# Strassen's seven products in the MLP down projection of a Griffin-style decoder layer

## Chip, cores and metric

The kernel runs on one core of a Trainium2 chip. The metric is device time in microseconds (us); the time of the kernel before is the median of three runs.

## The reference, cut to what matters

One decoder layer on 512 tokens of width 2048: three token mixers, a gated merge, and a squared-ReLU MLP with 8192 hidden features. All of it is float32. Only the MLP matters here:

```python
D_MODEL = 2048
SEQ = 512
D_FF = 4 * D_MODEL
...
        x = x + merged @ w_out[l]

        h2 = rms_norm(x, mlp_norm_w[l])
        x = x + jnp.square(jax.nn.relu(h2 @ w_mlp_up[l])) @ w_mlp_down[l]
```

## The kernel before

**Precision.** Each float32 factor is split into a high part (rounded to the fp32r type) and a low part (the rest). A product is three matmuls, high x high, high x low and low x high (`mm3`, lines 110 to 113). A weight tile arrives as `raw`, 128 partitions x 2 x 512 float32 (512 KB), by one load from SyncE's queue; ScalarE casts it to `whi` (line 100) and VectorE subtracts to get `wlo` (line 102). The rings hold 4 `raw`, 3 `whi` and 3 `wlo` tiles.

**MLP.** It runs in 8 blocks of 1024 hidden features (lines 923 to 941). The up product of a block is two calls of `feat_major`: 4 accumulators of 128 features x 512 tokens, 8 weight groups of 256 input features, so 24 matmuls of 128x128 by 512 columns for each weight tile. After each half, ScalarE applies relu (`rl`, line 929), VectorE squares (line 930), ScalarE casts to `u_h` (line 933), and VectorE subtracts to `u_l` (line 934). The factor of the second norm is left out of `u` and put into `r2` (one number for each token). The down product is four calls of `tok_major`, one for each 512 output columns: 4 accumulators of 128 tokens x 512 columns, 4 weight groups of 256 hidden features, again 24 matmuls for each weight tile. VectorE then adds each accumulator, times `r2`, to the residual `x1` (line 939). In the last block the results are stored right after that (line 941).

**Space.** Two pools of four PSUM tiles of 128 x 512: `acc` for the accumulators of both products, and `sm` for small things of the attention and for transposes. `T` is a pool of 75 tiles of 128 x 512 float32 in SBUF; in the MLP `x1` takes 16 of them, the normed activations `h2` 32, and `u_h` and `u_l` 16.

**Order.** The program is traced in the order written; the framework adds the semaphores and chooses each engine's order, in which an instruction can go ahead of an earlier one that is not yet ready. Once chosen, the order of each engine is fixed. The matmuls of one block's up and down products follow each other.

## Time and profile before

| what | us |
|---|---|
| median of three runs | 2969.28 (2967.07 to 2970.88) |
| span of the profiled execution | 2966.8 |
| TensorE busy | 2946.1 (99%) |
| VectorE busy | 1145.6 (39%) |
| ScalarE busy | 872.2 (29%) |
| MLP, first to last matmul (1569.6 to 2962.6 in the span) | 1393.0 |

For the profiled execution the profile gives its span only, from the first to the last recorded instruction; it is 2.5 us below the median of the runs. PE is TensorE's matmuls and PEld its weight loads, DVE is VectorE, ACT is ScalarE, POOL is GpSimd, SP is SyncE, whose queue issues the loads. A matmul's own duration (0.39 us) overlaps the next one's, so the spacing of the starts, not the duration, tells what one costs. In a row of a group, the text behind "|" gives busy us, the mean ns of one, and the idle time of the engine before them with what ended it.

### The profile page before, as it was taken

To read this page: it belongs to the slowest core of one execution; us is meant where nothing else is said; L and a number is where in the kernel's file an instruction comes from. 1 tells how busy PE (TensorE), PEld (TensorE's weight loads), DVE (VectorE), ACT (ScalarE), POOL (GpSimd) and SP (SyncE) were. 2 spreads that over 40 slices of the span, in tenths; PEclk is the share of its full clock that TensorE was granted. 3 is DMA by queue.
4 is the path that set the end of the run, shared out by engine and by line. 5 is a ranking of instruction groups with operands and counts; after the bars stand their busy time and mean duration, and the time that the engine had idled before them with its cause. 6 is when DMAs were issued, how large, how long until landed. Compare 5 with 4: busy or idle time off the path is not lost.

```text
span 2966.8 us, 33995 instructions
## 1 busy us (share of the span) xinstructions
PE 2946.1 (99%) x14046; PEld 2405.0 (81%) x14046; DVE 1145.6 (39%) x1697; ACT 872.2 (29%) x1352; POOL 125.1 (4%) x134
## 2 busy tenths in 40 slices
PE   8999999999999999999999999999999999999999
PEld 6988777777888888888888888888888888888887
DVE  6435666645322323343323333333332332433333
ACT  6334443344222222222323213122221312222131
POOL 0001111100000100010000000000000000000000
PEclk9999999999999999999999999999999999999999
DMA  6423222122333333333333333333333333333333
GB/s 228 119 71 87 65 68 66 54 65 65 95 97 100 93 99 100 93 98 111 113 119 93 99 94 99 98 94 100 95 97 100 93 99 100 93 100 96 96 100 106
DMA packets 198837, 285.97 MB, mean 96 GB/s; under 512 B 19575, under 2 KB 76698, under 8 KB 198682
## 3 DMA queue, kind: packets, MB, share of 16 engines
q1 hardware_dynamic: 189312, 281.16, 31.9%
q10 hardware_dynamic: 9370, 2.64, 0.4%
q8 instruction: 110, 1.80, 0.2%
q14 instruction: 45, 0.37, 0.0%
HBM read 279.16 MB, written 4.60 MB: 96 GB/s over the span
## 4 chain that ended last, share of the span: by engine, by line
PE 96%; DVE 1%; DMA 1%; POOL 1%; ACT 1%; issue 0%; ACTq 0%; SPq 0%; POOLq 0%; DVEq 0%
PE fa L111 20%; PE fa L112 20%; PE fa L113 20%; PE ta L113 10%; PE ta L111 10%; PE ta L112 10%; PE ps L802 1%; PE dps L795 1%; PE ps L810 1%; PE ps L789 0%; PE yy L754 0%; PE sp L493 0%; PE lp L561 0%; PE lp L517 0%; DVE wlo L102 0%
## 5 line engine op out<-in xcount | busy, mean ns | idle before, releaser
L102 DVE TENSOR_TENSOR wlo<-raw,whi 128x1024 fp32r<-128x1024 f32 (+2 forms) x520 | 626.7, 1206 | 1518.4 <-ACT whi L100 1514.8
L100 ACT CAST whi<-raw 128x1024 fp32r<-128x1024 f32 (+2 forms) x520 | 536.9, 1033 | 1682.7 <-PE fa L112 977.2
L111 PE MATMUL fa<-h_h,whi 128*128 128x512 f32 x2336 | 927.5, 397 | 0.0
L113 PE MATMUL fa<-h_h,wlo 128*128 128x512 f32 x2336 | 912.4, 391 | 0.0
L112 PE MATMUL fa<-h_l,whi 128*128 128x512 f32 x2336 | 912.4, 391 | 0.0
L111 PEld LDWEIGHTS fa<-h_h,whi 128*128 128x128 f32 x2336 | 438.6, 188 | 98.2 <-issue 11.3
L113 PEld LDWEIGHTS fa<-h_h,wlo 128*128 128x128 f32 x2336 | 438.5, 188 | 92.3 <-issue 1.0
L112 PEld LDWEIGHTS fa<-h_l,whi 128*128 128x128 f32 x2336 | 438.9, 188 | 86.6 <-issue 1.2
L111 PE MATMUL ta<-whi,u_h 128*128 128x512 f32 x1024 | 398.3, 389 | 0.0
L112 PE MATMUL ta<-wlo,u_h 128*128 128x512 f32 x1024 | 398.3, 389 | 0.0
L113 PE MATMUL ta<-whi,u_l 128*128 128x512 f32 x1024 | 398.3, 389 | 0.0
L113 PEld LDWEIGHTS ta<-whi,u_l 128*128 128x128 f32 x1024 | 192.2, 188 | 39.9
L111 PEld LDWEIGHTS ta<-whi,u_h 128*128 128x128 f32 x1024 | 192.2, 188 | 39.9
L112 PEld LDWEIGHTS ta<-wlo,u_h 128*128 128x128 f32 x1024 | 192.2, 188 | 39.9
L939 DVE SCALAR_TENSOR_TENSOR x<-ta,r,x 128x512 f32<-128x512 f32 x128 | 93.0, 747 | 44.2 <-PE ta L113 44.2
L111 PE MATMUL ta<-whi,m_h 128*128 128x512 f32 x256 | 99.9, 390 | 0.0
L113 PE MATMUL ta<-whi,m_l 128*128 128x512 f32 x256 | 99.6, 389 | 0.0
L112 PE MATMUL ta<-wlo,m_h 128*128 128x512 f32 x256 | 99.6, 389 | 0.0
L111 PE MATMUL fa<-ob_h,whi 128*128 128x512 f32 x256 | 99.6, 389 | 0.0
L112 PE MATMUL fa<-ob_l,whi 128*128 128x512 f32 x256 | 99.6, 389 | 0.0
L113 PE MATMUL fa<-ob_h,wlo 128*128 128x512 f32 x256 | 99.6, 389 | 0.0
L882 POOL TENSOR_TENSOR mg<-mg,sg 128x512 f32<-128x512 f32 x32 | 49.6, 1580 | 639.6 <-DVE sg L881 639.6
(279 smaller groups left out, 1912.0 us busy)
## 6 DMA issues: line engine op xcount, KB each, us to landing
raw<-in_w_mlp_up_dram SPq DMA_DIRECT2D x128, 512.0 KB, 3.7
raw<-in_w_mlp_down_dram SPq DMA_DIRECT2D x128, 512.0 KB, 3.8
raw<-in_w_in_dram SPq DMA_DIRECT2D x112, 512.0 KB, 3.6
raw<-in_w_in_dram SPq DMA_DIRECT2D x120, 256.0 KB, 3.0
raw<-in_w_out_dram SPq DMA_DIRECT2D x32, 512.0 KB, 3.8
raw<-in_w_mem_kv_dram SPq DMA_DIRECT2D x16, 512.0 KB, 4.9
raw<-in_p_swa_dram SPq DMA_DIRECT2D x12, 512.0 KB, 3.8
raw<-in_p_dn_dram SPq DMA_DIRECT2D x12, 512.0 KB, 3.8
```

The source lines that it names most:

```text
L100: nc.scalar.copy(out=hi, in_=raw)
L102: nc.vector.tensor_tensor(out=lo, in0=raw, in1=hi.bitcast(F32), op=ALU.subtract)
L111: nc.tensor.matmul(ps, lhsT=l_hi, rhs=r_hi, start=first, stop=False)
L112: nc.tensor.matmul(ps, lhsT=l_hi, rhs=r_lo, start=False, stop=False)
L113: last_mm[0] = nc.tensor.matmul(ps, lhsT=l_lo, rhs=r_hi, start=False, stop=last)
L795: nc.tensor.matmul(dps[rs, :], lhsT=R[rs, t, :], rhs=tmp, start=True, stop=True)
L802: nc.tensor.matmul(ps2, lhsT=kd[rs, t, :], rhs=delta, start=True, stop=True)
L810: nc.tensor.matmul(ps3[rs, :], lhsT=PT[rs, t, :], rhs=delta, start=True, stop=True)
L882: nc.gpsimd.tensor_tensor(out=merged[kt], in0=merged[kt], in1=sg[j], op=ALU.add)
L939: nc.vector.scalar_tensor_tensor(out=x1[t, c], in0=accs[t], scalar=r2[:, t:t + 1], in1=x1[t, c], op0=ALU.mult, op1=ALU.add)
```

## The change

In blocks 0 to 6 the down product (512 tokens x 1024 features by 1024 features x 2048 columns) is cut into halves in all three dimensions, 2x2 blocks of 256 x 512 and of 512 x 1024, and done by Strassen's method: seven block products of sums and differences. `SEVEN` lists for each product which activation blocks are combined, which weight blocks, and to which output blocks it goes with which sign. A weight block that is a sum is loaded as two `raw` tiles for each part and added by VectorE in place, ahead of the split. The activations are now kept unsplit as `u` (tiles of 128 x 2 x 256), with relu and square both on ScalarE; they are combined (`a_s`, VectorE) and split (`a_h` on ScalarE, `a_l` on VectorE) once for each product. A product is done in two units, one for each 512 columns: two accumulators from the `sm` pool, 24 matmuls, then an accumulation on VectorE into one or two output blocks for each of two token tiles, with `r2` or its negative and an add or a subtract for the sign.

Five of the seven products combine two weight blocks, five combine two activation blocks, and five go to two output blocks (twelve targets in all).

`merged_order` traces one up step of the next block (one weight tile, 24 matmuls), then one down unit of this block, and so on: 16 up steps with 14 units. Block 0's up product runs alone ahead, and block 7's down product stays the plain one behind, on four `sm` accumulators. The rest of the diff removes comments and names the ring's size of 4 (`RAWS`).

```diff
+RAWS = 4
+SEVEN = (
+    (((0, 0, 1),), ((0, 1, 1), (1, 1, -1)), ((0, 1, 1), (1, 1, 1))),
+    (((1, 1, 1),), ((1, 0, 1), (0, 0, -1)), ((0, 0, 1), (1, 0, 1))),
+    (((0, 0, 1), (1, 1, 1)), ((0, 0, 1), (1, 1, 1)), ((0, 0, 1), (1, 1, 1))),
+    (((1, 0, 1), (1, 1, 1)), ((0, 0, 1),), ((1, 0, 1), (1, 1, -1))),
+    (((0, 0, 1), (0, 1, 1)), ((1, 1, 1),), ((0, 0, -1), (0, 1, 1))),
+    (((1, 0, 1), (0, 0, -1)), ((0, 0, 1), (0, 1, 1)), ((1, 1, 1),)),
+    (((0, 1, 1), (1, 1, -1)), ((1, 0, 1), (1, 1, 1)), ((0, 0, 1),)),
+)
...
     NE = 8
-    for e_ in range(NE):
-        u = []
+    nr2 = const.tile([P, 4], F32, name="nr2")
+    nc.vector.tensor_scalar(out=nr2, in0=r2, scalar1=-1.0, scalar2=None, op0=ALU.mult)
+    sgn = {1: (ALU.add, r2), -1: (ALU.subtract, nr2)}
+    def up_steps(e_, u):
         for half in range(2):
-            accs = feat_major([rows(w_up, 256 * g, e_ * 1024 + half * 512, 512) for g in range(8)], h2, 4)
+            accs = [acc_tile("fa") for _ in range(4)]
+            for g in range(8):
+                hi, lo = wload(rows(w_up, 256 * g, e_ * 1024 + half * 512, 512), 512)
+                for j in range(4):
+                    for k in range(2):
+                        ah, al = h2[2 * g + k]
+                        c = slice(j * P, (j + 1) * P)
+                        mm3(accs[j], hi[:, k, c], lo[:, k, c], ah, al, g == 0 and k == 0, g == 7 and k == 1)
+                if g < 7:
+                    yield
             for j in range(4):
-                rl = T("rl")
-                nc.scalar.activation(out=rl, in_=accs[j], func=AF.Relu)
-                nc.vector.tensor_tensor(out=rl, in0=rl, in1=rl, op=ALU.mult)
-                hh = T("u_h", F32R)
-                hl = T("u_l", F32R)
-                nc.scalar.copy(out=hh, in_=rl)
-                nc.vector.tensor_tensor(out=hl, in0=rl, in1=hh.bitcast(F32), op=ALU.subtract)
-                u.append((hh, hl))
-        for c in range(4):
-            accs = tok_major([rows(w_dn, e_ * 1024 + 256 * g, c * 512, 512) for g in range(4)], u, 512, 4)
+                p_, k = 2 * half + j // 2, j % 2
+                for h in range(2):
+                    if k == 0:
+                        u[p_, h] = T("u", shape=(P, 2, 256))
+                    nc.scalar.activation(out=u[p_, h][:, k, :], in_=accs[j][:, h * 256:(h + 1) * 256], func=AF.Relu)
+                    if k == 1:
+                        nc.scalar.activation(out=u[p_, h], in_=u[p_, h], func=AF.Square)
+            yield
+    def split(src):
+        hh = T("a_h", F32R, (P, 2, 256))
+        hl = T("a_l", F32R, (P, 2, 256))
+        nc.scalar.copy(out=hh, in_=src)
+        nc.vector.tensor_tensor(out=hl, in0=src, in1=hh.bitcast(F32), op=ALU.subtract)
+        return hh, hl
+    def down_units(e_, u):
+        for at, bt, ct in SEVEN:
+            act = []
+            for i in range(2):
+                t0, k0, _ = at[0]
+                src = u[2 * k0 + i, t0]
+                if len(at) == 2:
+                    t1, k1, s1 = at[1]
+                    both = T("a_s", shape=(P, 2, 256))
+                    nc.vector.tensor_tensor(out=both, in0=src, in1=u[2 * k1 + i, t1], op=sgn[s1][0])
+                    src = both
+                act.append(split(src))
+            for c in range(2):
+                accs = [sm("da") for _ in range(2)]
+                for i in range(2):
+                    raws = []
+                    for k0, m0, _ in bt:
+                        raw = wp.tile([P, 2, 512], F32, tag="raw", bufs=RAWS, name="raw")
+                        nc.sync.dma_start(out=raw, in_=rows(w_dn, e_ * 1024 + k0 * 512 + i * 256, m0 * 1024 + c * 512, 512))
+                        raws.append(raw)
+                    if len(bt) == 2:
+                        nc.vector.tensor_tensor(out=raws[0], in0=raws[0], in1=raws[1], op=sgn[bt[1][2]][0])
+                    hi, lo = wsplit(raws[0], 512)
+                    ah, al = act[i]
+                    for t in range(2):
+                        for k in range(2):
+                            cs = slice(t * P, (t + 1) * P)
+                            mm3(accs[t], ah[:, k, cs], al[:, k, cs], hi[:, k, :], lo[:, k, :], i == 0 and k == 0, i == 1 and k == 1)
+                for t in range(2):
+                    for t0, m0, s0 in ct:
+                        tt, cc_ = 2 * t0 + t, 2 * m0 + c
+                        nc.vector.scalar_tensor_tensor(out=x1[tt, cc_], in0=accs[t], scalar=sgn[s0][1][:, tt:tt + 1], in1=x1[tt, cc_], op0=ALU.mult, op1=ALU.add)
+                yield
+    def merged_order(first_, second):
+        live = [first_, second]
+        while live:
+            for gen in list(live):
+                if next(gen, "end") == "end":
+                    live.remove(gen)
+    u = {}
+    for _ in up_steps(0, u):
+        pass
+    for e_ in range(NE - 1):
+        nu = {}
+        merged_order(up_steps(e_ + 1, nu), down_units(e_, u))
+        u = nu
+    us = {key: split(t_) for key, t_ in u.items()}
+    e_ = NE - 1
+    for c in range(4):
+        accs = [sm("da") for _ in range(4)]
+        for g in range(4):
+            hi, lo = wload(rows(w_dn, e_ * 1024 + 256 * g, c * 512, 512), 512)
             for t in range(4):
-                nc.vector.scalar_tensor_tensor(out=x1[t, c], in0=accs[t], scalar=r2[:, t:t + 1], in1=x1[t, c], op0=ALU.mult, op1=ALU.add)
-                if e_ == NE - 1:
-                    nc.sync.dma_start(out=out[0, t * P:(t + 1) * P, c * 512:(c + 1) * 512], in_=x1[t, c])
+                for k in range(2):
+                    ah, al = us[g, t // 2]
+                    cs = slice((t % 2) * P, (t % 2 + 1) * P)
+                    mm3(accs[t], ah[:, k, cs], al[:, k, cs], hi[:, k, :], lo[:, k, :], g == 0 and k == 0, g == 3 and k == 1)
+        for t in range(4):
+            nc.vector.scalar_tensor_tensor(out=x1[t, c], in0=accs[t], scalar=r2[:, t:t + 1], in1=x1[t, c], op0=ALU.mult, op1=ALU.add)
+            nc.sync.dma_start(out=out[0, t * P:(t + 1) * P, c * 512:(c + 1) * 512], in_=x1[t, c])
```

## Rows read from the trace of the kernel before

**Rows 1.** Page: busy time by engine, granted clock in 40 slices, chain by engine.

```profile
PE 2946.1 (99%) x14046; PEld 2405.0 (81%) x14046; DVE 1145.6 (39%) x1697; ACT 872.2 (29%) x1352; POOL 125.1 (4%) x134
...
PEclk9999999999999999999999999999999999999999
...
PE 96%; DVE 1%; DMA 1%; POOL 1%; ACT 1%; issue 0%; ACTq 0%; SPq 0%; POOLq 0%; DVEq 0%
```

**Rows 2.** Windows, the MLP: stretch, length, busy us by engine, clock, DMA, GB/s.

```profile
1569.60:2962.60 1393.00, 1393.00 (x6148) 1153.19 (x6146) 484.96 (x516) 339.57 (x387) 0.00 (x0) 1.00 0.32 97
```

**Rows 3.** Waits of TensorE, whole span: total us, times, longest; ten rows there.

```profile
PE vps L79 <- DMA vm<-in_mem_norm_w_dram: 6.2, 1, 6.2
...
PE kv L112 <- DVE wlo L102: 1.9, 3, 1.1
...
PE kv L111 <- ACT hm_h L144: 0.2, 1, 0.2
```

**Rows 4.** Timeline of TensorE at a seam: start, us; 18 matmuls apart.

```profile
2262.09 0.39 PE L111 MATMUL ta<-whi,u_h 128*128 128x512 f32 x1
...
2266.17 0.39 PE L111 MATMUL fa<-h_h,whi 128*128 128x512 f32 x1
```

**Rows 5.** Groups of VectorE and ScalarE from 1540 us on.

```profile
L102 DVE TENSOR_TENSOR wlo<-raw,whi 128x1024 fp32r<-128x1024 f32 x259 | 317.3, 1225 | 852.4 <-ACT whi L100 850.2
L939 DVE SCALAR_TENSOR_TENSOR x<-ta,r,x 128x512 f32<-128x512 f32 x128 | 93.0, 747 | 44.2 <-PE ta L113 44.2
L934 DVE TENSOR_TENSOR u_l<-rl,u_h 128x512 fp32r<-128x512 f32 x64 | 44.2, 691 | 33.0 <-ACT u_h L933 33.0
L930 DVE TENSOR_TENSOR rl<-rl 128x512 f32<-128x512 f32 x64 | 43.9, 685 | 0.0
L100 ACT CAST whi<-raw 128x1024 fp32r<-128x1024 f32 x259 | 272.9, 1054 | 1002.5 <-PE ta L113 543.0 <-PE fa L112 459.4
L933 ACT CAST u_h<-rl 128x512 fp32r<-128x512 f32 x64 | 39.8, 622 | 49.2 <-DVE rl L930 49.2
L929 ACT ACTIVATE rl<-fa 128x512 f32<-128x512 f32 x64 | 38.0, 594 | 8.5 <-PE fa L113 8.5
L903 ACT ACTIVATE jk<-x 128x512 bf16<-128x512 f32 x4 | 2.5, 626 | 2.5 <-DVE x L902 2.5
```

**Rows 6.** Timeline of VectorE at the same seam, a down block's end.

```profile
2256.58 1.22 DVE L102 TENSOR_TENSOR wlo<-raw,whi 128x1024 fp32r<-128x1024 f32 x1 [4.21 <-ACT whi L100]
2262.02 1.23 DVE L102 TENSOR_TENSOR wlo<-raw,whi 128x1024 fp32r<-128x1024 f32 x1 [4.21 <-ACT whi L100]
2263.16 1.40 DVE L939 SCALAR_TENSOR_TENSOR x<-ta,r,x 128x512 f32<-128x512 f32 x2
...
2266.37 0.75 DVE L939 SCALAR_TENSOR_TENSOR x<-ta,r,x 128x512 f32<-128x512 f32 x1 [0.61 <-PE ta L113]
2267.46 1.23 DVE L102 TENSOR_TENSOR wlo<-raw,whi 128x1024 fp32r<-128x1024 f32 x1 [0.34 <-ACT whi L100]
```

**Rows 7.** Timeline of ScalarE at the same seam, with the idle time before.

```profile
2266.37 1.06 ACT L100 CAST whi<-raw 128x1024 fp32r<-128x1024 f32 x1 [4.38 <-PE ta L113]
```

**Rows 8.** Page, DMA issues: count, KB each, median us to landing.

```profile
raw<-in_w_mlp_down_dram SPq DMA_DIRECT2D x128, 512.0 KB, 3.8
...
x<-in_x_dram SPq DMA_DIRECT2D x16, 256.0 KB, 6.1
```

**Rows 9.** Windows of earlier stages with a busy VectorE or DMA.

```profile
30.00:36.00 6.00, 5.76 (x22) 3.54 (x21) 3.68 (x9) 5.84 (x17) 0.56 (x1) 1.00 1.05 381
40.00:50.00 10.00, 7.53 (x31) 5.46 (x31) 7.27 (x15) 9.90 (x26) 1.26 (x2) 1.00 0.62 231
50.00:60.00 10.00, 9.74 (x43) 7.75 (x42) 8.47 (x18) 8.84 (x29) 2.02 (x3) 1.00 0.55 167
300.00:310.00 10.00, 10.00 (x95) 8.37 (x94) 7.51 (x17) 5.96 (x15) 1.91 (x2) 1.00 0.41 105
```

**Rows 10.** Timeline of VectorE: two operations that follow directly.

```profile
47.86 2.35 DVE L102 TENSOR_TENSOR wlo<-raw,whi 128x1024 fp32r<-128x1024 f32 x2
```

More of the change, by code (lines that the diff above doesn't have):

```diff
@@ L89, in wload @@
     def wload(src, n):
-        raw = wp.tile([P, 2, n], F32, tag="raw", bufs=4, padded_shape=[P, 2, 512], name="raw")
+        raw = wp.tile([P, 2, n], F32, tag="raw", bufs=RAWS, padded_shape=[P, 2, 512], name="raw")
         if len(src.shape) == 3:
@@ L376, in tile_layer @@
     for g in range(8):
-        raw = wp.tile([P, 2, 268], F32, tag="raw", bufs=4, padded_shape=[P, 2, 512], name="raw")
+        raw = wp.tile([P, 2, 268], F32, tag="raw", bufs=RAWS, padded_shape=[P, 2, 512], name="raw")
         nc.sync.dma_start(out=raw[:, :, 0:12], in_=rows(w_in, 256 * g, COL_BA, 12))
```

## The prediction, made before the changed kernel was run

> **What bounds the kernel now.** I read the busy shares and the granted clock first [rows 1]: TensorE is busy 99% of a 2966.8 us span, VectorE 39%, ScalarE 29%, the clock stands at full (2.4 GHz) in every slice, and the chain of waits is 96% TensorE. A busy TensorE need not be a full one, so I read its waits next [rows 3]: the ten rows of that view add up to 15.9 us, all of them in the prologue, the key/value projection and the attention before the MLP; no row is from an MLP line. Then the MLP alone [rows 2]: 1393.0 us from its first matmul to its last, TensorE busy in all of it, VectorE 485.0 us, ScalarE 339.6 us, DMA at 0.32 of its engines and 97 GB/s. It holds 8 x (384 up + 384 down) = 6144 matmuls, so 1393.0/6144 = 0.2267 us each; the stream shows the same spacing, (2266.17 - 2262.09)/18 = 0.2267 us [rows 4], across the seam from a down to an up product. So the MLP's time is its matmul count times 0.2267 us. Fewer matmuls are worth that each, as long as nothing else becomes late.
>
> **What is removed.** A down block has 4 column chunks x 4 feature groups x 4 token tiles x 2 x 3 = 384 matmuls. The seven products have 7 x 2 x 2 x 2 x 2 x 3 = 336, of the same 128x128 by 512 shape. That is 48 fewer in each of 7 blocks, 336 x 0.2267 = 76.2 us. The eighth block is unchanged. All of it lies on the path that sets the end.
>
> The Trainium skill, page "TensorE: Matmul & The Clock Gate", section "Back-to-back issue gap", gives about 131 ns for a matmul of 512 columns in a sustained stream with weight loads; by that the removal would be worth 336 x 0.131 = 44 us. The trace disagrees with its 0.2267 us, so the trace decides.
>
> **What is added, engine by engine.** The block is now 16 up steps and 14 down units of 24 matmuls, 24 x 0.2267 = 5.44 us each: 30 x 5.44 = 163.2 us for what took 32 x 5.44 = 174.1. Everything below has to fit beside it.
>
> VectorE [rows 5]: per block before, 32 weight subtractions x 1.225 + 8 squares x 0.685 + 8 activation subtractions x 0.691 + 16 accumulations x 0.747 = 62.2 us. After: 16 + 28 = 44 weight subtractions (53.9), 20 sums of two weight blocks (five products x 4; not in the trace, nearest is the weight subtraction of the same shape, 1.225, so 24.5), 10 sums and 14 subtractions of activations at 0.69 (16.6), and 12 targets x 4 = 48 accumulations x 0.747 (35.9): 130.9 us of 163.2, 80%. The load is uneven. In the third product a pair (one up step, one down unit, 10.88 us) carries 1 + 2 + 2 operations of 1.225, four accumulations and two activation operations: 6.13 + 2.99 + 1.38 = 10.5 us, 96%. Durations overlap when operations follow directly: two weight subtractions took 2.35 us [rows 10], so the second cost 1.13, and two accumulations took 1.40 [rows 6], 0.65 for the second. With these the pair is 5 x 1.13 + 4 x 0.65 + 2 x 0.69 = 9.6 us, 88%. I take 9.6, because a queue this full has its operations back to back.
>
> The Trainium skill, page "VectorE: DVE Perf Modes", section "The DRAIN you can't avoid", speaks against this: a next operation does not start before the pipe of the last is empty. By it the pair stays at 10.5 of 10.88 us and leaves almost no room. The two rows with 2.35 and 1.40 show an overlap, so I keep 9.6.
>
> ScalarE [rows 5]: 44 casts x 1.054 + 14 activation casts x 0.622 + 16 half-width relus at no more than 0.594 + 8 squares x 0.626 = 69.6 us of 163.2; before it was 32 x 1.054 + 8 x 0.594 + 8 x 0.622 = 43.5. Nothing is tight here. Square, relu and cast all stand among the six ScalarE groups of the stretch from 1540 us on, of which the rows show four, and a table load is not among the six, so I cost none.
>
> DMA: 16 + 48 = 64 loads of 524,288 bytes per block instead of 32, 33.6 MB in 163.2 us = 206 GB/s; in the first three and the last two products five loads in 10.88 us = 241 GB/s. In the prologue the same queue moved 381 GB/s [rows 9], so the engines can carry it. The load ring has 4 tiles. A load lands after 3.8 us [rows 8]; one that holds a sum is then added (1.23), cast (1.05) and subtracted (1.23): 7.3 us. Five loads through 4 slots need a slot to turn in 4/5 x 10.88 = 8.7 us. It fits by 1.4 us, and the second block of a sum frees its slot at the addition. On SyncE's queue the up and down loads stand in the order of use; only the last block's output stores follow them, as now. A slot that waits longer because the cast waits for TensorE to release a weight tile is ahead of need, not late.
>
> **What hides it.** Three split weight tiles are in flight. The cast's idle time of 4.38 us ends at TensorE [rows 7], so it waits for a release, one to two groups ahead of need. VectorE's order at a seam is the row that matters most [rows 6]: the next block's first two subtractions (2256.58, 2262.02) stand ahead of the four accumulations (from 2263.16), the third (2267.46) behind them, and TensorE crossed the seam at 2266.17 without a gap. In the changed kernel an up step is 5.44 us and half a unit 2.72 us, so three tiles still cover 10.88 us of matmuls. A subtraction that comes 5 us late costs nothing.
>
> **Terms that are not zero.** TensorE waits in the MLP cannot fall below the zero they have now, so these have no gain side. For a full VectorE the nearest rows are two windows [rows 9]: 7.51 of 10 us busy and TensorE at 10.00; 8.47 of 10 and TensorE at 9.74, 2.6% lost. I apply 2.6% to the third product alone, 7 x 2 x 10.88 = 152 us: 4.0 us. The upper bound is the first three products, 457 us: 11.9 us. At the last block all eight activation tiles are split before its plain down product; the first half's tiles can be split during the last up steps. I take 1 us, bounds 0 and 5 (four 0.622 casts and four 0.69 subtractions in a row). The accumulations of a unit now run beside the next up step; the unit's two PSUM tiles are wanted again only two units later, so that 10.88 us cover their 1.4 us.
>
> **Sum.** 2966.8 - 76.2 + 4.0 + 1.0 = 2895.6 us of span. The median of the runs, 2969.28, is 2.5 us above the span, so 2898.
>
> **Rivals.** (1) Head of the line on VectorE. If a unit's accumulations stand in VectorE's queue ahead of the next up step's subtraction, TensorE has only the two matmuls (0.45 us) that need no low part. The accumulations of the last token tile wait for the unit's end: 1.40 + 1.23 - 0.45 = 2.2 us lost for a product with two targets, 0.75 + 1.23 - 0.45 = 1.5 with one. Ten and four units in seven blocks: 7 x (10 x 2.2 + 4 x 1.5) = 196 us, so 2969 - 76 + 196 = 3089, slower. It decides from 76.2/98 units = 0.78 us per unit on. For it: VectorE is in order and doubles its load. Against it: [rows 6], where the subtractions go ahead. (2) A part of it: VectorE late in the dense stretches by 0.3 to 0.6 us per unit, 29 to 59 us, 2922 to 2952. For it: the window with VectorE at 7.27 and ScalarE at 9.90 of 10 us left TensorE 7.53 [rows 9]. Against: there ScalarE was full, and here it is not. (3) The load ring. A load lands in 6.1 us where many are queued [rows 8]; then a slot turns in 9.6 us, a dense pair takes 5/4 x 9.6 = 12.0, and 10 dense pairs x 7 blocks x 1.1 = 79 us, so 2969 - 76 + 79 = 2972, no change. It decides from a turn of 8.7 us on. Against it: at most four loads are outstanding, not sixteen. (4) That the change does not do what it says, namely that a product costs more than 48 matmuls of the usual spacing, has nothing in the trace for it: same shapes, same engine, both operand roles as now.
>
> **How the numbers follow.** My forecast (stalls of 0 to 20 us, 2889 to 2915) has 0.66, rival (2) 0.15, (1) 0.13, (3) and (4) together 0.06. Of (3) most lies within 0.2%, which is about what a measurement of this kernel can tell from no change (6 us). So faster 0.81, same 0.05, slower 0.14. The forecast's own range is 2889 to 2915; to hold 8 in 10 the range must take in rival (2), and 3 us below for the spread of the runs: 2886 to 2955.
>
> **What would show it.** The three matmul lines that write the new accumulators should have 912 instructions each, with the spacing still 0.2267 us. VectorE should be near 80% in a merged block (130.9 us by durations, somewhat less where operations overlap), the window's DMA near 206 GB/s, the total bytes near 286 + 7 x 32 x 0.524 = 403 MB. Waits of TensorE on MLP lines should add up to under 20 us and end at the weight subtraction. If (1) holds, these waits are on the up product's third matmul, released by VectorE, 98 times at about 2 us; if (3), SyncE's waits shrink and the weight sums wait for DMA. My forecast is wrong if TensorE's waits in the MLP exceed 20 us or the spacing of the matmuls has changed.

## The result, and the profile after

The changed kernel takes 2914.72 us, median of four runs (2913.22 to 2924.87), beside 2968.18 us for the kernel before on the same chip. The ratio is 0.9824, with a 95% interval of 0.9809 to 0.9840. It is faster by 53.5 us; the forecast was 71 (2969.28 - 2898).

The page of the kernel after: busy time by engine with instruction counts, the granted clock, the bytes moved, the chain by engine, then groups by line (count | busy us, mean ns of one | idle before, releaser) and the landing time of the down loads.

```profile
span 2911.4 us, 34617 instructions
...
PE 2880.4 (99%) x13710; PEld 2341.0 (80%) x13710; DVE 1569.0 (54%) x2194; ACT 1016.0 (35%) x1606; POOL 125.1 (4%) x134
...
PEclk9999999999999999999999999999999999999999
...
DMA packets 259773, 403.47 MB, mean 139 GB/s; under 512 B 23159, under 2 KB 80282, under 8 KB 259610
...
PE 87%; DVE 5%; DMA 5%; ACT 1%; issue 1%; POOL 1%; SPq 0%; ACTq 0%; DVEq 0%; POOLq 0%
...
L124 PE MATMUL da<-wlo,a_h 128*128 128x512 f32 x912 | 358.9, 393 | 7.9 <-DVE wlo L114 7.8
...
L991 DVE TENSOR_TENSOR raw<-raw 128x1024 f32<-128x1024 f32 x140 | 171.2, 1223 | 174.2 <-DMA raw<-in_w_mlp_down_dram 174.0
...
L1001 DVE SCALAR_TENSOR_TENSOR x<-da,r,x 128x512 f32<-128x512 f32 x280 | 195.7, 742 | 0.2 <-PE da L125 0.2
...
raw<-in_w_mlp_down_dram SPq DMA_DIRECT2D x352, 512.0 KB, 4.1
```

From the view of VectorE's waits (total us, times, longest):

```profile
DVE raw L991 <- DMA raw<-in_w_mlp_down_dram: 174.0, 105, 4.9
```

14046 matmuls have become 13710, 336 fewer, and the clock stands at full as in [rows 1]. TensorE is still "99% busy", so that figure shows nothing of what was lost. The chain does: TensorE's share of it fell from 96% [rows 1] to 87%, and VectorE and DMA have 5% each. The row of L991, the sum of two weight blocks, names both: VectorE stood idle 174.0 us in front of 105 of its 140 sums, waiting for a load of the down weights.

How much TensorE lost is read from starts, not from busy time. The timeline of TensorE in the kernel after (start, duration), at the MLP's first and last matmul:

```profile
1569.51 0.48 PE L123 MATMUL fa<-h_h,whi 128*128 128x512 f32 x1
...
2906.92 0.39 PE L125 MATMUL da<-whi,a_l 128*128 128x512 f32 x1
```

The MLP has 8 x 384 up, 7 x 336 and 384 down matmuls, 5808. At the spacing of [rows 4] their starts would span 5807 x 0.2267 = 1316.4 us; they span 2906.92 - 1569.51 = 1337.4. So 21.0 us were lost, where before none were [rows 2, 3]. The view of TensorE's waits in the MLP shows only half of it (total us, times, longest):

```profile
PE da L124 <- DVE wlo L114: 7.8, 10, 1.3
PE fa L125 <- DVE wlo L114: 2.6, 4, 1.3
```

A matmul's duration in the records is 0.39 us and the spacing 0.2267, so a gap of less than 0.16 us shows as no idle time. What the view does show is the releaser: always the weight subtraction on VectorE, in an up step (L125, `fa`) and in a down unit (L124, `da`).

Windows of the kernel after, one block (length, busy us by engine, clock, DMA share, GB/s):

```profile
1992.00:2158.00 166.00, 164.92 (x725) 135.53 (x724) 122.18 (x136) 63.38 (x85) 0.00 (x0) 1.00 0.64 204
...
2003.00:2014.00 11.00, 9.92 (x44) 7.88 (x43) 10.49 (x14) 4.61 (x6) 0.00 (x0) 1.00 0.62 191
...
2036.00:2047.00 11.00, 11.00 (x48) 8.76 (x48) 8.62 (x10) 3.18 (x4) 0.00 (x0) 1.00 0.73 229
2047.00:2058.00 11.00, 11.00 (x50) 9.07 (x49) 9.46 (x11) 4.98 (x5) 0.00 (x0) 1.00 0.77 255
```

Of the eleven-microsecond windows the one that lost (2003 to 2014) holds the block's second unit. The third product (2036 to 2058), where the forecast had put its stalls, shows no loss in its two windows; counted by starts over the seven merged blocks, its two pairs of up step and unit lost 4.4 us and the block's second pair 8.9, 0.8 to 1.6 in each block. In the second unit the stall returns some 166 us apart in six of the blocks (2007.30, 2172.25, 2338.04, ...; in the first block it falls in the up step before), and the one at 2338 looks like this. Timeline of the kernel after, VectorE first, then ScalarE, then TensorE; in brackets the idle time before and its releaser:

```profile
2331.79 1.23 DVE L991 TENSOR_TENSOR raw<-raw 128x1024 f32<-128x1024 f32 x1 [1.14 <-DMA raw<-in_w_mlp_down_dram]
2332.93 0.69 DVE L966 TENSOR_TENSOR a_l<-a_s,a_h 128x512 fp32r<-128x512 f32 x1
2333.53 0.68 DVE L979 TENSOR_TENSOR a_s<-u 128x512 f32<-128x512 f32 x1
2334.13 2.72 DVE L1001 SCALAR_TENSOR_TENSOR x<-da,r,x 128x512 f32<-128x512 f32 x4
2336.77 2.35 DVE L114 TENSOR_TENSOR wlo<-raw,whi 128x1024 fp32r<-128x1024 f32 x2
...
2334.25 0.62 ACT L965 CAST a_h<-a_s 128x512 fp32r<-128x512 f32 x1 [3.13 <-DVE a_s L979]
2334.78 1.04 ACT L112 CAST whi<-raw 128x1024 fp32r<-128x1024 f32 x1
...
2336.40 0.39 PE L123 MATMUL da<-whi,a_h 128*128 128x512 f32 x1
2338.04 0.50 PE L124 MATMUL da<-wlo,a_h 128*128 128x512 f32 x1 [1.25 <-DVE wlo L114]
```

The sum waited 1.14 us for its second load. Behind it stood two activation operations, four accumulations and the subtraction that TensorE needed: it started at 2336.77, though its cast had ended at 2335.82, and that cast was itself late, behind an activation cast that waited for the same queue. TensorE lost 2338.04 - 2336.40 - 0.2267 = 1.41 us. From this one place three causes are possible: the loads are late, VectorE is full, or its order is bad.

### The profile page after: what moved, and what is told of

It reads as the page before. It is cut to its first block, busy times and chain, and to the rows that moved or that the text cites. A ratio compares the mean times of both kernels' runs of the same rounds, so it can differ in the third digit from the quotient of the medians.

```text
span 2911.4 us, 34617 instructions
## 1 busy us (share of the span) xinstructions
PE 2880.4 (99%) x13710; PEld 2341.0 (80%) x13710; DVE 1569.0 (54%) x2194; ACT 1016.0 (35%) x1606; POOL 125.1 (4%) x134
## 2 busy tenths in 40 slices
DMA packets 259773, 403.47 MB, mean 139 GB/s; under 512 B 23159, under 2 KB 80282, under 8 KB 259610
## 4 chain that ended last, share of the span: by engine, by line
PE 87%; DVE 5%; DMA 5%; ACT 1%; issue 1%; POOL 1%; SPq 0%; ACTq 0%; DVEq 0%; POOLq 0%
PE fa L123 19%; PE fa L125 19%; PE fa L124 19%; PE da L124 6%; PE da L125 6%; PE da L123 5%; DMA raw<-in_w_mlp_down_dram 4%; PE ta L123 2%; PE ta L124 2%; PE ta L125 2%; DVE wlo L114 2%; DVE raw L991 2%; DVE x L1001 1%; PE dps L807 1%; PE ps L814 1%
## 5 line engine op out<-in xcount | busy, mean ns | idle before, releaser
L114 DVE TENSOR_TENSOR wlo<-raw,whi 128x1024 fp32r<-128x1024 f32 (+2 forms) x604 | 723.2, 1205 | 909.5 <-ACT whi L112 906.4
L112 ACT CAST whi<-raw 128x1024 fp32r<-128x1024 f32 (+2 forms) x604 | 621.9, 1035 | 1434.6 <-PE fa L124 709.2
L125 PE MATMUL fa<-h_h,wlo 128*128 128x512 f32 x2336 | 913.6, 391 | 2.7 <-DVE wlo L114 2.6
L124 PE MATMUL fa<-h_l,whi 128*128 128x512 f32 x2336 | 912.8, 391 | 0.0
L125 PEld LDWEIGHTS fa<-h_h,wlo 128*128 128x128 f32 x2336 | 438.7, 188 | 97.2 <-DVE wlo L114 5.3
L124 PEld LDWEIGHTS fa<-h_l,whi 128*128 128x128 f32 x2336 | 439.1, 188 | 86.6 <-issue 1.2
L124 PE MATMUL da<-wlo,a_h 128*128 128x512 f32 x912 | 358.9, 393 | 7.9 <-DVE wlo L114 7.8
L123 PE MATMUL da<-whi,a_h 128*128 128x512 f32 x912 | 355.4, 390 | 0.2
L125 PE MATMUL da<-whi,a_l 128*128 128x512 f32 x912 | 355.1, 390 | 0.0
L991 DVE TENSOR_TENSOR raw<-raw 128x1024 f32<-128x1024 f32 x140 | 171.2, 1223 | 174.2 <-DMA raw<-in_w_mlp_down_dram 174.0
L124 PEld LDWEIGHTS da<-wlo,a_h 128*128 128x128 f32 x912 | 171.2, 188 | 54.5 <-DVE wlo L114 19.7
L123 PEld LDWEIGHTS da<-whi,a_h 128*128 128x128 f32 x912 | 171.3, 188 | 36.9 <-ACT a_h L965 1.0
L125 PEld LDWEIGHTS da<-whi,a_l 128*128 128x128 f32 x912 | 171.3, 188 | 34.4
L1001 DVE SCALAR_TENSOR_TENSOR x<-da,r,x 128x512 f32<-128x512 f32 x280 | 195.7, 742 | 0.2 <-PE da L125 0.2
L125 PE MATMUL ta<-whi,m_l 128*128 128x512 f32 x256 | 99.7, 389 | 0.0
L124 PE MATMUL ta<-wlo,m_h 128*128 128x512 f32 x256 | 99.7, 389 | 0.0
L124 PE MATMUL fa<-ob_l,whi 128*128 128x512 f32 x256 | 99.6, 389 | 0.0
L125 PE MATMUL fa<-ob_h,wlo 128*128 128x512 f32 x256 | 99.6, 389 | 0.0
```

The lines of the kernel that those rows point to most:

```text
L112: nc.scalar.copy(out=hi, in_=raw)
L114: nc.vector.tensor_tensor(out=lo, in0=raw, in1=hi.bitcast(F32), op=ALU.subtract)
L123: nc.tensor.matmul(ps, lhsT=l_hi, rhs=r_hi, start=first, stop=False)
L124: nc.tensor.matmul(ps, lhsT=l_hi, rhs=r_lo, start=False, stop=False)
L125: last_mm[0] = nc.tensor.matmul(ps, lhsT=l_lo, rhs=r_hi, start=False, stop=last)
L991: nc.vector.tensor_tensor(out=raws[0], in0=raws[0], in1=raws[1], op=sgn[bt[1][2]][0])
```

## The experiments

Each kernel was timed in three rounds beside the kernel before on the same chip (2968.1 to 2969.1 us); the ratio is to that. Without any loss the time would be 2968.5 - 76.2 = 2892.3 us. In the expectations A is the theory that the loads are short of ring slots; B that the activation work at a block's start is in the way; C that a late load hurts only where VectorE's queue is full; D, formed after the first eight of these runs, that VectorE's fixed order puts a sum which waits for its second load ahead of a subtraction that TensorE needs next.

**Six ring slots instead of four.**

```diff
-N_SLOTS = 75
+N_SLOTS = 71
-RAWS = 4
+RAWS = 6
```

> The changed kernel with 6 weight tiles in the load ring instead of 4, and 71 tiles in the activation pool instead of 75 to make room. Theory A (the ring of 4 loads is too short: sums of weight blocks wait for their second load, and the 21 us that the MLP lost to waits come from there): the loss falls to 3 us or less, 2894 to 2898 us. Theory B (order at the start of a block: casts stand behind activation casts and subtractions behind accumulations on engines that go in order): unchanged, 2911 to 2916 us, with the wait of about 1.4 us at each block's second unit still there.

Measured 2904.24 us (2903.39 to 2905.78), ratio 0.9783 (0.9769 to 0.9798): about half of the loss came back, which is neither theory. In the profiled run, the slowest of its four, 14.2 us are still lost by starts. TensorE's waits that remain (first), and one of them on VectorE, ScalarE and TensorE, in the traces of this kernel:

```profile
PE da L124 <- DVE wlo L114: 5.6, 6, 2.1
PE fa L125 <- DVE wlo L114: 4.2, 5, 1.3
```

```profile
2489.30 1.23 DVE L991 TENSOR_TENSOR raw<-raw 128x1024 f32<-128x1024 f32 x1 [2.80 <-DMA raw<-in_w_mlp_down_dram]
2490.45 1.22 DVE L114 TENSOR_TENSOR wlo<-raw,whi 128x1024 fp32r<-128x1024 f32 x1
...
2487.69 1.05 ACT L112 CAST whi<-raw 128x1024 fp32r<-128x1024 f32 x1 [0.53 <-PE da L125]
...
2490.44 0.39 PE L124 MATMUL fa<-h_l,whi 128*128 128x512 f32 x1
2491.72 0.50 PE L125 MATMUL fa<-h_h,wlo 128*128 128x512 f32 x1 [0.89 <-DVE wlo L114]
```

The cast was done at 2488.74 and VectorE was idle, yet the subtraction started at 2490.45: the sum in front of it stood 2.80 us waiting for its load. VectorE is not full here: it was busy 8.20 of the 11 us from 2482 to 2493. This row is where theory D comes from, though it was put in words only later.

**The second load of each sum left out** (the sum adds a block to itself, so VectorE keeps its work).

```diff
-                    for k0, m0, _ in bt:
+                    for k0, m0, _ in bt[:1]:
...
-                        nc.vector.tensor_tensor(out=raws[0], in0=raws[0], in1=raws[1], op=sgn[bt[1][2]][0])
+                        nc.vector.tensor_tensor(out=raws[0], in0=raws[0], in1=raws[0], op=sgn[bt[1][2]][0])
```

> The changed kernel, but a weight block that is a sum is loaded once and added to itself: the second load is left out (20 of 64 loads of a block), every operation on the engines stays. Theory A (loads): the loss of 21 us falls to 3 us or less, 2894 to 2898 us. Theory B (order on VectorE and ScalarE): the 1.4 us at each block's second unit stay, 7 x 1.4 = 10 us, so 2903 to 2908 us.

Measured 2892.46 us (2890.72 to 2895.00), ratio 0.9744 (0.9728 to 0.9761), a little below even A's range. The view shows no wait of TensorE in the MLP, and by starts 0.7 us is lost. The same row of VectorE from 1580 us on:

```profile
L991 DVE TENSOR_TENSOR raw<-raw 128x1024 f32<-128x1024 f32 x140 | 167.3, 1220 | 68.4 <-DMA raw<-in_w_mlp_down_dram 68.4
```

VectorE had the same operations at the same durations (124.58 us busy in the window 1992 to 2158, 75%), and next to nothing was lost: such a load costs nothing by itself. The loss goes with the second load; how the load causes it, this run doesn't tell.

**The sum on 16 of its 1024 columns,** with both loads kept.

```diff
-                        nc.vector.tensor_tensor(out=raws[0], in0=raws[0], in1=raws[1], op=sgn[bt[1][2]][0])
+                        nc.vector.tensor_tensor(out=raws[0][:, :, 0:8], in0=raws[0][:, :, 0:8], in1=raws[1][:, :, 0:8], op=sgn[bt[1][2]][0])
```

> The changed kernel, but the sum of two weight blocks is done on 16 of its 1024 columns only: both loads stay and are waited for, VectorE is relieved of about 1.06 us for each of 20 sums in a block (21 us, 13% of its time). Theory A (loads): most of the loss stays, 2906 to 2915 us. Theory B (VectorE's load and order): the loss falls below 6 us, 2894 to 2900 us.

Measured 2902.93 us (2900.00 to 2904.23), ratio 0.9777 (0.9762 to 0.9791): between the theories. VectorE from 1580 us on:

```profile
L991 DVE TENSOR_TENSOR raw<-raw 128x16 f32<-128x16 f32 x140 | 24.6, 176 | 337.7 <-DMA raw<-in_w_mlp_down_dram 337.6
```

With 147 us of VectorE work gone (171.2 to 24.6), the wait for the loads doubled and TensorE still lost some 11 us. A faster VectorE comes to the waiting sum earlier. The order changed too: here every sum stands ahead of one or two subtractions that TensorE needs earlier, in the change 56 of 140 do (counted below), so the run does not price VectorE's work alone.

**The activation sums on GpSimd.**

```diff
-                    nc.vector.tensor_tensor(out=both, in0=src, in1=u[2 * k1 + i, t1], op=sgn[s1][0])
+                    nc.gpsimd.tensor_tensor(out=both, in0=src, in1=u[2 * k1 + i, t1], op=sgn[s1][0])
```

> The changed kernel with the ten activation sums of a block on GpSimd, which does nothing in the MLP, instead of VectorE. Theory A (loads): unchanged, 2911 to 2916 us. Theory B: the activation cast no longer waits for VectorE's queue in front of the weight cast; the wait at each block's second unit shrinks or goes, 2901 to 2907 us.

Measured 2931.33 us (2928.30 to 2939.05), ratio 0.9878 (0.9862 to 0.9894): 17 us slower than the change. GpSimd's sum, then VectorE's activation subtraction and accumulation in the same kernel:

```profile
L979 POOL TENSOR_TENSOR a_s<-u 128x512 f32<-128x512 f32 x70 | 109.0, 1570 | 1258.8 <-ACT u L959 776.5 <-DVE wlo L114 156.1 <-PE da L124 122.7
...
L966 DVE TENSOR_TENSOR a_l<-a_s,a_h 128x512 fp32r<-128x512 f32 x70 | 55.3, 807 | 15.0 <-ACT a_h L965 15.0
L1001 DVE SCALAR_TENSOR_TENSOR x<-da,r,x 128x512 f32<-128x512 f32 x280 | 195.7, 742 | 3.9 <-PE da L125 3.9
```

A sum takes 1570 ns there (684 on VectorE), and VectorE's subtraction grew from 685 to 807 ns. Two things changed at once, so the run doesn't settle B; it shows that GpSimd is no relief here. The order of the sums stayed nearly that of the change (count below).

**One target for each product:** for the five products with two targets the second one's accumulations are left out, 20 of 48 in a block.

```diff
-                    for t0, m0, s0 in ct:
+                    for t0, m0, s0 in ct[:1]:
```

> The changed kernel with every product accumulated into its first output block only: 20 of the 48 accumulations of a block are left out (13 us of VectorE), all loads and sums stay. Theory A (loads alone: the second load of a sum is late because the ring is short): the loss of 21 us stays, 2908 to 2915 us. Theory C (a late load hurts only where VectorE's queue is full behind it, that is in the first three products, which have two targets and two loads; the last two have two loads, one target and no loss): the loss falls below 6 us, 2892 to 2899 us.

Measured 2974.58 us (2971.17 to 2979.05), ratio 1.0023 (1.0014 to 1.0033). A kernel with less work in it is 60 us slower than the change, against A and C both. TensorE's waits in the MLP, VectorE's row, and one stall on VectorE, ScalarE and TensorE:

```profile
PE fa L125 <- DVE wlo L114: 45.2, 34, 2.6
PE da L124 <- DVE wlo L114: 12.0, 20, 1.1
```

```profile
L991 DVE TENSOR_TENSOR raw<-raw 128x1024 f32<-128x1024 f32 x140 | 171.6, 1226 | 368.5 <-DMA raw<-in_w_mlp_down_dram 368.5
```

```profile
2207.08 1.22 DVE L114 TENSOR_TENSOR wlo<-raw,whi 128x1024 fp32r<-128x1024 f32 x1
2211.77 1.23 DVE L991 TENSOR_TENSOR raw<-raw 128x1024 f32<-128x1024 f32 x1 [3.47 <-DMA raw<-in_w_mlp_down_dram]
2212.91 1.22 DVE L114 TENSOR_TENSOR wlo<-raw,whi 128x1024 fp32r<-128x1024 f32 x1
...
2207.11 1.06 ACT L112 CAST whi<-raw 128x1024 fp32r<-128x1024 f32 x1 [1.23 <-PE fa L124]
...
2212.76 0.39 PE L124 MATMUL fa<-h_l,whi 128*128 128x512 f32 x1
2214.19 0.50 PE L125 MATMUL fa<-h_h,wlo 128*128 128x512 f32 x1 [1.04 <-DVE wlo L114]
```

The cast was ready at 2208.17. The subtraction behind it could have run then, in VectorE's idle time; it ran at 2212.91, after the sum. TensorE's order is the same in both kernels. VectorE's is not. The tiles are numbered in the order in which they were traced, which is the order in which TensorE uses them, so from the order of VectorE's instructions one can count how many subtractions that TensorE needs earlier stand behind a sum in VectorE's queue:

```
sums with ... earlier-needed subtractions behind them   0    1    2    3    4
the change                                             84   46   10    -    -
six ring slots                                          -   21   63   45   11
second load left out                                    -   42   82   16    -
sum on 16 columns                                       -  124   16    -    -
activation sums on GpSimd                              76   54   10    -    -
one target                                              -  130   10    -    -
another order of the products (below)                  77   53   10    -    -
ordering rule for the sum (below)                     140    -    -    -    -
```

In the change 56 of 140 sums stand ahead of something more urgent, in the kernel with one target all of them. With accumulations left out, the framework chose another order. That made D the theory to test.

**Another order of the seven products** (those without a weight sum put between those with one).

```diff
     (((0, 0, 1),), ((0, 1, 1), (1, 1, -1)), ((0, 1, 1), (1, 1, 1))),
+    (((1, 0, 1), (0, 0, -1)), ((0, 0, 1), (0, 1, 1)), ((1, 1, 1),)),
+    (((1, 0, 1), (1, 1, 1)), ((0, 0, 1),), ((1, 0, 1), (1, 1, -1))),
     (((1, 1, 1),), ((1, 0, 1), (0, 0, -1)), ((0, 0, 1), (1, 0, 1))),
-    (((0, 0, 1), (1, 1, 1)), ((0, 0, 1), (1, 1, 1)), ((0, 0, 1), (1, 1, 1))),
-    (((1, 0, 1), (1, 1, 1)), ((0, 0, 1),), ((1, 0, 1), (1, 1, -1))),
     (((0, 0, 1), (0, 1, 1)), ((1, 1, 1),), ((0, 0, -1), (0, 1, 1))),
-    (((1, 0, 1), (0, 0, -1)), ((0, 0, 1), (0, 1, 1)), ((1, 1, 1),)),
+    (((0, 0, 1), (1, 1, 1)), ((0, 0, 1), (1, 1, 1)), ((0, 0, 1), (1, 1, 1))),
```

> The changed kernel with the seven products in another order (first, sixth, fourth, second, fifth, third, seventh of the list), so that no two products with two weight blocks and two targets follow each other; work, loads and rings are the same. Theory C: the loss of 21 us falls to 5 to 12 us, 2898 to 2906 us. Theory A: unchanged, 2911 to 2916 us, as the loads of a block are the same.

Measured 2908.47 us (2903.95 to 2910.71), ratio 0.9795 (0.9781 to 0.9810). It lies between what the theories gave and tells nothing apart. By the count above, the sums stand nearly as in the change.

**The weight sums on GpSimd.**

```diff
-                        nc.vector.tensor_tensor(out=raws[0], in0=raws[0], in1=raws[1], op=sgn[bt[1][2]][0])
+                        nc.gpsimd.tensor_tensor(out=raws[0], in0=raws[0], in1=raws[1], op=sgn[bt[1][2]][0])
```

> The changed kernel with the 20 sums of weight blocks on GpSimd instead of VectorE: a sum that waits for its load no longer stands in front of VectorE's other work and VectorE has 24 us less in a block, but a sum takes about 3.1 us (twice the 1.57 us that 512 columns took there) instead of 1.22. Theory C (VectorE's order): the gain of a free queue should win, 2893 to 2905 us. Theory A (the time of a tile in the ring): 1.9 us more for each turn of 7.3, so worse, 2915 to 2950 us.

Measured 3107.78 us (3103.20 to 3108.63), ratio 1.0466 (1.0450 to 1.0481), slower than any theory said. GpSimd's row, and TensorE's longest wait in this kernel:

```profile
L991 POOL TENSOR_TENSOR raw<-raw 128x1024 f32<-128x1024 f32 x140 | 343.4, 2453 | 1262.9 <-DMA raw<-in_w_mlp_down_dram 1254.1 <-DVE wlo L114 8.7
```

```profile
PE da L123 <- ACT whi L112: 90.3, 49, 3.2
```

The wait moved to the next in-order queue: ScalarE's casts waited 676.2 us for these sums, and then TensorE for the casts. The sum takes twice as long on GpSimd, 2453 ns. Which part of the 215 us is the slower sum and which the order of ScalarE was not separated. A third part is the clock: the mean granted clock was 0.982 (0.999 with the rule below), and 204 matmuls in stretches at the lower level (1.2 GHz) started some 0.43 us apart instead of 0.2267, an estimated 41 us.

**The two streams apart:** all down units of a block, then the next block's up steps.

```diff
-        merged_order(up_steps(e_ + 1, nu), down_units(e_, u))
+        for _ in down_units(e_, u):
+            pass
+        for _ in up_steps(e_ + 1, nu):
+            pass
```

> The seven products without the interleave: a block's down units run one after the other, then the next block's up product. What the interleave hides, by the prediction's durations: a unit has 5.44 us of matmuls and 6.1 to 8.4 us of VectorE, an excess of about 23 us in a block, 164 us in seven. 3040 to 3100 us.

Measured 3142.43 us (3141.60 to 3147.48), ratio 1.0589 (1.0573 to 1.0605). Seven products without the interleaving lose 3142 - 2892 = 250 us and are slower than eight; the change loses 21. The direction was expected, the size was more than the 3040 to 3100 given. TensorE's two longest waits:

```profile
PE da L123 <- ACT whi L112: 80.6, 86, 2.8
PE da L124 <- DVE wlo L114: 47.0, 48, 3.1
```

The clock has a part in it. A window of this kernel (length, busy us by engine, clock, DMA, GB/s):

```profile
1681.90:1688.70 6.80, 4.55 (x11) 3.58 (x12) 5.33 (x6) 1.04 (x1) 0.00 (x0) 0.50 0.72 229
```

After a stretch with waits, TensorE busy in 16.69 of 21.9 us, the granted clock fell to its lower level, 1.2 GHz. The mean clock was 0.980, which is some 126 us at half speed; 236 matmuls in such stretches started 0.43 us apart instead of 0.2267, an estimated 47 us. Without these the time would be about 3095, inside the range given.

**An ordering rule for the sum alone.** The sum goes into VectorE's queue behind the weight subtraction that was traced last; loads, operations and ring stay as in the change.

```diff
+    last_lo = [None]
...
-        nc.vector.tensor_tensor(out=lo, in0=raw, in1=hi.bitcast(F32), op=ALU.subtract)
+        last_lo[0] = nc.vector.tensor_tensor(out=lo, in0=raw, in1=hi.bitcast(F32), op=ALU.subtract)
...
-                        nc.vector.tensor_tensor(out=raws[0], in0=raws[0], in1=raws[1], op=sgn[bt[1][2]][0])
+                        with tc.issue_after(last_lo[0].ins):
+                            nc.vector.tensor_tensor(out=raws[0], in0=raws[0], in1=raws[1], op=sgn[bt[1][2]][0])
```

> The changed kernel with one ordering rule: on VectorE, a sum of two weight blocks may not stand ahead of the weight subtractions traced before it. Work, loads and rings are the same. Theory D (the loss is VectorE standing at a sum whose second load has not landed, with a subtraction that TensorE needs next queued behind it): the waits of TensorE for subtractions shrink, 2893 to 2902 us. Theory A (the ring is short, whatever the order): 2908 to 2915 us.

Measured 2893.07 us (2891.88 to 2896.78), ratio 0.9750 (0.9734 to 0.9766); the view shows no wait of TensorE in the MLP. The MLP's first and last matmul, the sum's row (line 995 here), a stretch of VectorE, and the windows of one block and of its first 11 us:

```profile
1568.04 0.47 PE L126 MATMUL fa<-h_h,whi 128*128 128x512 f32 x1
...
2885.57 0.39 PE L128 MATMUL da<-whi,a_l 128*128 128x512 f32 x1
```

```profile
L995 DVE TENSOR_TENSOR raw<-raw 128x1024 f32<-128x1024 f32 x140 | 171.0, 1222 | 56.9 <-DMA raw<-in_w_mlp_down_dram 56.2
```

```profile
2335.82 2.36 DVE L117 TENSOR_TENSOR wlo<-raw,whi 128x1024 fp32r<-128x1024 f32 x2 [0.60 <-ACT whi L115]
2340.20 1.23 DVE L995 TENSOR_TENSOR raw<-raw 128x1024 f32<-128x1024 f32 x1 [2.02 <-DMA raw<-in_w_mlp_down_dram]
```

```profile
2153.00:2319.00 166.00, 166.00 (x734) 137.31 (x733) 125.53 (x141) 64.15 (x84) 0.00 (x0) 1.00 0.62 206
...
2153.00:2164.00 11.00, 11.00 (x50) 9.13 (x49) 10.94 (x14) 4.30 (x5) 0.00 (x0) 1.00 0.62 202
```

A sum still waits for its load, here 2.02 us, but behind the two subtractions and not ahead of them. No sum stands ahead of an earlier-needed subtraction now (last line of the count). The ring has four tiles, VectorE does the same work at the same rate, and the loss is gone: the starts span 2885.57 - 1568.04 = 1317.5 us, 1.1 more than without any loss, where the change lost 21.0. That is D. VectorE was busy 10.94 of 11.00 us in the last window shown and TensorE did not wait, so a full VectorE is not the cause. Nor is the activation work (B) by itself: apart from the sums, the rule moved four operations of a block on VectorE and one cast on ScalarE, by one to three places, and nothing on TensorE or in SyncE's queue.

**The rule with six ring slots.** The edits of the rule and of the six slots together.

```diff
+RAWS = 6
...
+                        with tc.issue_after(last_lo[0].ins):
```

> The same ordering rule with 6 tiles in the load ring and 71 in the activation pool. Theory D and theory A each explain a part of what the ring of 6 left (about 11 us above 2893): with the rule 2893 to 2898 us; if the rest had another cause than the order on VectorE, 2902 to 2906 us as with the ring of 6 alone.

Measured 2891.86 us (2891.22 to 2893.66), ratio 0.9743 (0.9728 to 0.9757). The difference to the rule alone (0.9750, 0.9734 to 0.9766) is within both intervals: with the order right, the ring of four costs nothing that can be measured.

**The rule, six slots, and the activation work in order too.**

```diff
+                    with tc.issue_after(last_lo[0].ins):
+                        nc.vector.tensor_tensor(out=both, in0=src, in1=u[2 * k1 + i, t1], op=sgn[s1][0])
...
+                with tc.issue_after(last_hi[0].ins):
+                    act.append(split(src))
```

> As the last, and the activation sums, casts and subtractions may not stand ahead of the weight subtractions and casts traced before them either. If the activation work that runs ahead at the start of a block is what fills VectorE and ScalarE there, 2893 to 2896 us and less than the last; if the activations now come late for their product, 2900 to 2925 us with TensorE waiting for activation casts.

Measured 2892.14 us (2891.44 to 2892.94), ratio 0.9743 (0.9728 to 0.9757). Nothing more is gained, and there was nothing left: with the sums in order, the activations' order does not matter.

**One target, with the rule.** The slowest of the orders, with the sum held back.

```diff
-                    for t0, m0, s0 in ct:
+                    for t0, m0, s0 in ct[:1]:
...
+                        with tc.issue_after(last_lo[0].ins):
```

> The kernel with one accumulation target for each product (20 of 48 accumulations of a block left out), which took 2974.6 us, with the ordering rule of the sums added. Theory D (its 82 us of waits are sums that stand ahead of subtractions in VectorE's order): 2890 to 2897 us. If the early sums were only a sign of loads that come late for another reason: above 2930 us.

Measured 2891.41 us (2890.72 to 2894.78), ratio 0.9739 (0.9723 to 0.9755). One rule of order takes 2974.58 to 2891.41, 83 us, at the same loads and the same work. The view shows no wait of TensorE in the MLP, and by starts 0.7 us is lost. In these two kernels the orders of TensorE, ScalarE and SyncE's queue are the same; on VectorE only the sums and five other operations of a block stand in other places.

## Why the prediction was right, and where it was off

**The removal: right to within the measurement.** 336 x 0.2267 = 76.2 us was the size of the gain. The page has 336 matmuls fewer and 912 on each of the three lines; with the order mended the gain is 2968.53 - 2893.07 = 75.5 us. The spacing did not change. The Trainium skill's rule of the page "TensorE: Matmul & The Clock Gate", section "Back-to-back issue gap", by which an estimated 44 us would have gone, does not hold for this stream.

**The stalls: mis-sized, 21.0 us instead of 5.0.** This is the step that failed, "Terms that are not zero". It priced a full VectorE from two windows of another stage [rows 9] and placed the price, 4.0 us, in the third product. The second load's removal and the ordering rule showed that the same VectorE work, 122 to 126 us of a block's 166, costs nothing. The place was wrong as well: most was lost in the block's second pair (8.9 us) and elsewhere. That the third product lost 4.4 us, near the 4.0, is luck: with the rule, at the same VectorE work, 0.4 is left there. What stalls is not a shortage of VectorE time but time in which it stands still at the head of its queue.

**What VectorE carries: right.** 130.9 us by durations with "somewhat less where operations overlap" is 122.18 and 125.53 us in the two windows shown. Two subtractions in 2.35 us and four accumulations in 2.72 us bear out the overlap of [rows 6, 10], and by the same rows the wait that the Trainium skill describes (page "VectorE: DVE Perf Modes", section "The DRAIN you can't avoid") does not show here; that section itself lets an operation that is not held start earlier. ScalarE has 63.4 us for 69.6 foreseen.

**The ring: right about the slots, wrong about what follows.** "It fits by 1.4 us" holds in the sense that it was asked: with four slots and the right order TensorE lost 1.1 us. But the working took a sum as one step of a slot's turn. A sum needs two loads, so it holds two slots and, once it is at the head, VectorE as well, until the second has landed: 174.0 us in all, in a queue where nothing can go ahead. Six slots brought half of the loss back, though by the count every sum then stood ahead of one to four subtractions: the sums waited less (150.0 us instead of 174.0 on VectorE's row of that kernel) in a worse order. Leaving out the second load made the order worse too (one to three) and cost nothing, though the sums still waited 68.4 us: a bad order costs only when the operation at the head waits, and not every such wait reaches TensorE. Rival (3)'s sign, weight sums that wait for DMA, showed, but a load landed after 4.1 us and not the 6.1 that it needs, and with the rule the sums wait 56.2 us and nearly nothing is lost. The bytes (403.47 MB) and the rate (204 GB/s of 206) were right.

**"A subtraction that comes 5 us late costs nothing": this cover was taken for granted at the new seams.** The order of VectorE was rightly called the row that matters most, and rival (1) had the right mechanism, the head of the line. It had the wrong head. It named the accumulations, which hardly wait: 0.2 us before the 280 of L1001 that the page groups. The waiting head was the sum, an operation that the trace of before could not show, and whose wait the prediction never priced. In size it came to 21.0/98 = 0.21 us for each unit, below rival (2)'s 0.3 to 0.6; in the one-target kernel, (2974.58 - 2892.3)/98 = 0.84, past the 0.78 from which rival (1) gives the whole gain back, and that kernel is indeed no faster than before, though the accumulations that rival (1) names are the work left out there.

**The bounds named beforehand.** "Under 20 us" of waits was just missed when counted by starts (21.0), and met in the view of waits (10.4), which hides the short ones. "End at the weight subtraction" was right. The range of 2886 to 2955 held the time, and so did the forecast's own, at its upper edge: 2914.72 in 2889 to 2915. That it did so is luck: two of the four runs lie above it, and the largest stalls were of a kind that the sum has no term for.

**What stays open.** Why second loads are still late with six slots (2.80 us in the row shown) was not tested; with six slots and the rule no sum waits for a load, so it goes with sums that stand early. Nor was the share of ScalarE's order in the 215 us of the weight sums on GpSimd tested. That the streams apart lost more than was expected is explained by the clock as an estimate only.

## What to carry to other kernels

Where an in-order engine gets an operation that waits for a transfer, ask what stands behind it in the queue: its price is the time in which ready work waits, not its own duration, and an engine at 75% can starve another while it is idle. Such a loss shows as idle time of the waiting row released by DMA, together with a later row whose input was ready long before; it is mended by an ordering rule, while a faster engine or more buffers took back only half of it here, and less work made it worse. Count lost time from starts where durations overlap.

## What the runs showed of the hardware

- Leaving out 20 of 48 accumulations in a block made the kernel 60 us slower, and one rule of order took that away again. A time that moves against the work is a sign of a changed order.
- A sum of two 128x512 fp32 tiles takes 1570 ns on GpSimd and 684 on VectorE; at 128x1024 it is 2453 and 1223. Beside GpSimd's sums VectorE's activation subtraction grew from 685 to 807 ns (1020 beside the weight sums), while its accumulation, which reads one of its tiles from PSUM, stayed at 742. The Trainium skill, page "SBUF — State Buffer", section "SBUF: two separate sides", says that a VectorE operation with two SBUF inputs and a GpSimd operation that reads SBUF exclude each other; these rows agree. With the weight sums on GpSimd, VectorE's activation subtractions that met none of them, or began before one, took 0.68 to 0.69 us, and those that began more than 0.26 us after one 1.1 to 2.9 us; the activation sum on VectorE stayed at 684 ns, as only 8 of its 70 met a GpSimd sum, and none of these began more than 0.26 us after it.
- A load of 512 KB landed after 3.8 us before [rows 8], 4.1 in the change, 4.4 with the rule, and 4.8 with six slots (medians): the longer ring came with longer landings, as did some kernels with four slots (4.6 with one target and the rule).
